# Twelve-tile down projections computed two columns at a time, and the first layer's last two column groups one at a time

## The chip, the cores and the metric

The kernel runs on one core of one Trainium2 chip. The metric is device time in microseconds, the median of several executions. Engines have the profile's names: PE is TensorE (matrix products; PEld its weight loads), DVE is VectorE, ACT is ScalarE, POOL is GpSimd, SP is SyncE, which issues the weight transfers.

## The reference

An encoder trunk of two layers on 256 tokens with 2048 features, all in float32. The first layer mixes tokens by attention, the second by a gated linear recurrence; both end in the same gated feed-forward, which the change is about:

```python
x = x + mixer(rms_norm(x, norm_mix))
x = x + (jax.nn.silu(h @ w_gate) * (h @ w_up)) @ w_down    # h = rms_norm(x, norm_ffn)
# x: 256 x 2048; w_gate, w_up: 2048 x 5632; w_down: 5632 x 2048
```

The second layer's recurrent mixer begins with `rms_norm` of the first layer's result and the projection `h @ w_in`.

## The kernel before

**Products.** Every float32 operand is held as two parts, `hi` and `lo` (the rest). A product of a 128x128 activation tile with a 128x512 weight tile is three matmuls: hi by hi, hi by lo, lo by hi (`product`, L289 to L296). The 256 tokens are two blocks `a` of 128; the accumulator of one block and 512 columns fills one PSUM bank, and the pool `ps_a` has four such banks, handed out in turn.

**Weight tiles.** One weight transfer (`half()`, `load_half`) brings 512 KB: two 128-row slices of 512 columns, which is one *step* of one *column group*. ScalarE casts it to `hi` (L123), VectorE subtracts to get `lo` (L124); there are five buffers each for the raw tile, `hi` and `lo`. One weight tile feeds four products (two slices, two token blocks), that is 12 matmuls of 128x512.

**Pairs.** `project_pair` computes two column groups `j` = 0, 1 together, in a list of steps. A step is a number `n` and the columns it serves: the first steps serve both, one after the other, the last ones first finish column 0 and then column 1, so that column 0's `done` (adding its two banks into the result) runs beside column 1's products. In the steps named in `SEVEN` (2 and 5) both columns' weight tiles are combined and seven products do the work of eight (`seven_forms`, L251 to L274): VectorE makes weight sums (`wx`, L264 to L267), ScalarE and VectorE split them (`wxh` L271, `wxl` L272), and at the end `merge` (L331 to L337) puts four further banks (`pm`, pool `ps_m`) together. The activation sides of these products (`x_forms`, tiles `nf` and `hf`) are prepared when the activation tiles are.

**Feed-forward.** The 5632 hidden features are 44 tiles, computed in parts of 12, 16 and 16 (`PARTS`). For each part, *units* of four hidden tiles are computed first: one pair whose columns are gate and up. A unit's end (L783 to L787, then `turned` and L795, L796) adds the banks, applies SiLU and the product, transposes the block (DVE, L462), copies it together in 16 pieces (ACT, L470: tile `tf` from `tb`) and splits the four hidden tiles (`act`: hi by ACT L795, lo by DVE L796). Then the part's *down projection* adds its share to the residual `x_tok`, in four column groups of 512.

- A sixteen-tile part (eight steps) uses `down`: two pairs (columns 0 and 1, then 2 and 3), with seven products in steps 2 and 5.
- The twelve-tile part (six steps) uses `output`, which is also what the mixers' output projections use: column after column, each by `project_tokens` (matmuls on L247), with two banks per column, all eight products in every step; the result is added on L498.

In the third part the second pair follows `LAST_STEPS`, in which step 3 comes before step 2.

**The end of the first layer.** The third part's `down` also prepares the next norm: as each column is done, `norm.add` squares it on ACT (`nj`, L426), transposes and copies it (L462, L468 on DVE, L470 on ACT; the buffers `tb` and `tf` are single) and writes four operand tiles `xg` (hi ACT L418, lo DVE L419). After the last column, `norm.finish` and `spread` compute the row factors (`nrt`, `nr`, `ndg` L444, a small product L450, the copy `nrb` L452). TensorE meanwhile runs `project_two`: the first two output columns of `w_in`, first over the eight operand tiles of columns 0 and 1, then those of column 2, then those of column 3. Their result passes through a convolution on DVE and ACT (`cb` L827, L829, L832) into `xs` (L378, L379), which the recurrence's gate products read (`pm<-xs,ghi`). The gates' weights (`graw`, L855) are loaded into memory that the feed-forward has just given up; ACT and POOL split them (`ghi` L856, `glo` L857).

**What sets the order.** TensorE's instructions stand in the order of the code. Those of the other engines and of the transfer queue are put in order by a scheduler that plays the program through with its own times; each engine then works strictly in that order.

Of the kernel before, what the change touches and what calls it, by code (L numbers as in the profile page):

```python
# [21 lines left out]
KT = D // P  # L22
# [8 lines left out]
FIRST_STEPS = (0, 1, 3, 4, 2, 6, 5, 7)  # L31
LAST_STEPS = (0, 1, 3, 2, 4, 5, 6, 7)
HALF = 8
# [40 lines left out]
def trunk(ctx, tc, w, out):  # L74
# [64 lines left out]
    def unit_steps(first):  # L139
        return FIRST_STEPS if first else USUAL_STEPS, True  # L140

    def down_steps(p, second):
        last = p == len(PARTS) - 1
        return LAST_STEPS if second and last else USUAL_STEPS, True

    def ffn_order(l):
        units = [wide(f"w_gate{l}"), wide(f"w_up{l}")]
        seq, i = [], 0
        for p, n in enumerate(PARTS):
            for _ in range(n // FOUR):  # L150
                for k, cols in pair_plan(*unit_steps(i == 0)):
# [135 lines left out]

    def project_pair(xs, forms, order, middle, done):
        banks = [[new_acc() for _ in range(2)] for _ in range(2)]  # L289
        begun = set()  # L290

        def product(acc, x, wt, last=False):
            for i, (a, b) in enumerate(((x[0], wt[0]), (x[0], wt[1]), (x[1], wt[0]))):
                pe.matmul(acc, a, b, start=id(acc) not in begun, stop=last and i == 2)  # L294
# [7 lines left out]
        steps = pair_plan(*order)  # L302
        seven = [n for n in order[0] if n in forms]
        for n, cols in steps:
            if n in forms:
                s1, s2, s3, s4 = forms[n]
                b11, b21, t3, b22, t1, t2, t4 = seven_forms()
                if n == seven[0]:
                    p1, q6, q5, q7 = (ps_m.tile([P, WIDE], F32, tag="pm", name=nm("pm")) for _ in range(4))
                last = n == seven[-1]  # L310
                product(p1, tokens(2 * n, 0), b11, last)
                product(banks[0][0], tokens(2 * n + 1, 0), b21)
                product(banks[1][0], s4, b22)
# [3 lines left out]
                product(banks[0][1], tokens(2 * n + 1, 1), t4)  # L317
                if last:
                    middle(p1, q5, q6, q7)
            else:  # L320
                for j in cols:
                    half()
                    hi, lo = (flat(t) for t in newest["tiles"])
                    end = n == order[0][-1]
                    for a in range(2):
                        for k in range(2):
                            product(banks[j][a], tokens(2 * n + k, a), (hi[:, k, :], lo[:, k, :]), end and k == 1)
                    if end:
                        done(j, banks[j])

# [175 lines left out]

    def down(xs, forms, p, norm=None, end=False):
        for c in (0, 2):
# [18 lines left out]

            project_pair(xs, forms, down_steps(p, c > 0), middle, done)
        if norm is not None:
# [245 lines left out]
    def ffn(norm, nxt):  # L775
        def unit(hid, forms, first):
            got = []
# [10 lines left out]

            project_pair(norm.xs, norm.forms, unit_steps(first), lambda *banks: got.extend(merge(*banks)), done)
            u = got[1]  # L790
# [7 lines left out]
            for i, n in enumerate(SEVEN):  # L798
                if forms is not None and first <= 2 * n < len(hid):
                    forms[n] = x_forms(hid[2 * n], hid[2 * n + 1], f"hf{i}")  # L800

        for p, n in enumerate(PARTS):
            hid, forms = [], {} if n == KT else None
            for i in range(n // FOUR):
                unit(hid, forms, p == i == 0)
            last = p == len(PARTS) - 1
            if last and nxt is not None:
                ln_exp_tables()
            if n == KT:
                down(hid, forms, p, nxt if last else None, last and nxt is None)  # L810
            else:
                output(hid)

# [220 lines left out]
```

## Time and profile before

| | |
|---|---|
| median of three runs | 2022.96 us (2022.78 to 2024.07) |
| profiled execution: its own time | 2022.37 us |
| profiled execution: span from first to last instruction | 2020.6 us |
| mean granted clock of TensorE | 0.993 |
| HBM read | 382.13 MB, 190 GB/s over the span |

Rows of the profile that the prediction quotes have these forms. *Waits*: the waiting engine, tile and line, what it waited for; total us, number of waits, longest. *Windows*: start and end from the span's start, length, then busy us (and instructions) of PE, PEld, DVE, ACT, POOL, the granted clock (1.00 is full), the busy share of the DMA engines, GB/s. *Timeline*: start, duration, engine, line, operation, output from inputs, shape, count, and in brackets the idle time before it and what ended it. *Chain*: start, duration and count of one piece of the chain of work that ended last.

### The profile page before, as it was taken

How to read it: one execution, taken by the hardware profiler on the slowest of the kernel's cores; microseconds unless marked ns; L12 is line 12 of the kernel's file. 1: busy time of each engine (PE TensorE's matmuls, PEld its weight loads, DVE VectorE, ACT ScalarE, POOL GpSimd, SP SyncE). 2: the span in 40 equal slices, each digit the busy share in tenths (PEclk: the TensorE clock that was granted, in tenths of full speed). 3: DMA queues.
4: the chain of work that ended last, by engine and by line, in shares of the span. 5: the costliest groups of instructions: out<-in, count | busy, mean ns of one | idle time of the engine just before them, and what ended most of it. 6: DMA issues, size and time to landing. Idle time of an engine off the chain costs nothing.

```text
span 2020.6 us, 27860 instructions
## 1 busy us (share of the span) xinstructions
PE 1995.2 (99%) x9944; PEld 1696.2 (84%) x9944; DVE 1666.0 (82%) x2347; ACT 1320.7 (65%) x2054; POOL 165.7 (8%) x213
## 2 busy tenths in 40 slices
PE   9999999999999999999899999999999999999999
PEld 8898888878888888887799998888788888888887
DVE  8998788856888888889868887898657898878897
ACT  7666666644667546677688898667545766457663
POOL 1463000000000000000133330000000000000000
PEclk9999999999999999999999999999999999999999
DMA  8444665656555665555555555655566566665564
GB/s 320 158 137 140 193 200 187 207 168 198 192 195 187 219 208 188 190 195 192 188 163 188 178 179 174 200 188 187 195 185 202 185 204 206 203 192 187 196 222 146
DMA packets 109004, 386.06 MB, mean 191 GB/s; under 512 B 12225, under 2 KB 12993, under 8 KB 108737
## 3 DMA queue, kind: packets, MB, share of 16 engines
q1 hardware_dynamic: 108720, 384.26, 58.0%
q8 instruction: 78, 1.28, 0.3%
q14 instruction: 62, 0.50, 0.1%
q10 hardware_dynamic: 144, 0.02, 0.0%
HBM read 382.13 MB, written 2.10 MB: 190 GB/s over the span
## 4 chain that ended last, share of the span: by engine, by line
PE 52%; issue 41%; DVE 4%; DMA 1%; ACT 1%; POOL 0%; DVEq 0%; SPq 0%; ACTq 0%; POOLq 0%
PE acc L294 24%; PE acc L247 7%; PE acc L225 6%; PE pm L294 4%; PE acc L341 3%; PE acc L342 3%; PE acc L343 3%; DVE lo L124 2%; PE pm L342 1%; PE pm L343 1%; PE pm L341 1%; DMA raw<-in_w_up_dram 1%; ACT hi L123 0%; DMA graw<-in_w_gates_dram 0%; ACT tf L470 0%
## 5 line engine op out<-in xcount | busy, mean ns | idle before, releaser
L123 ACT CAST hi<-raw 128x1024 fp32r<-128x1024 f32 (+1 forms) x708 | 730.4, 1045 | 486.1 <-PE acc L294 314.1
L124 DVE TENSOR_TENSOR lo<-raw,hi 128x1024 fp32r<-128x1024 f32 (+1 forms) x708 | 857.4, 1228 | 172.0 <-ACT hi L123 169.9
L294 PE MATMUL acc<-hi,xg 128*128 128x512 f32 x2200 | 694.4, 389 | 2.3 <-DVE fg L783 1.2
L294 PEld LDWEIGHTS acc<-hi,xg 128*128 128x128 f32 x2200 | 412.9, 188 | 91.0 <-DVE fg L783 2.0
L294 PE MATMUL acc<-lo,xg 128*128 128x512 f32 x1100 | 427.9, 389 | 0.0
L247 PE MATMUL acc<-hi,act 128*128 128x512 f32 x896 | 283.4, 395 | 6.2 <-ACT act L795 5.4
L294 PE MATMUL acc<-hi,act 128*128 128x512 f32 x800 | 252.7, 389 | 0.0
L294 PEld LDWEIGHTS acc<-lo,xg 128*128 128x128 f32 x1100 | 206.5, 188 | 42.4
L247 PEld LDWEIGHTS acc<-hi,act 128*128 128x128 f32 x896 | 170.7, 191 | 43.8 <-ACT act L795 6.3
L470 ACT COPY tf<-tb 32x256 f32<-32x256 f32 x448 | 180.8, 403 | 12.7 <-DVE tb L462 6.1
L294 PEld LDWEIGHTS acc<-hi,act 128*128 128x128 f32 x800 | 150.2, 188 | 32.3 <-issue 0.7
L247 PE MATMUL acc<-lo,act 128*128 128x512 f32 x448 | 176.8, 395 | 0.0
L294 PE MATMUL acc<-lo,act 128*128 128x512 f32 x400 | 155.6, 389 | 0.0
L342 PE MATMUL acc<-xg,hi 128*128 128x256 f32 x512 | 146.7, 286 | 2.0 <-DVE xg L419 1.9
L341 PE MATMUL acc<-xg,hi 128*128 128x256 f32 x512 | 146.8, 287 | 1.0 <-ACT xg L418 1.0
L343 PE MATMUL acc<-xg,lo 128*128 128x256 f32 x512 | 146.2, 285 | 0.0
L264 DVE TENSOR_TENSOR wx<-raw,raw 128x512 f32<-128x512 f32 x60 | 41.5, 692 | 123.7 <-DMA raw<-in_w_up_dram 97.1
L225 PE MATMUL acc<-xg,hi 128*128 128x512 f32 x384 | 127.1, 400 | 0.5 <-ACT hi L123 0.5
L271 ACT CAST wxh<-wx 128x1536 fp32r<-128x1536 f32 x60 | 88.9, 1482 | 49.6 <-DVE wx L267 46.7
L272 DVE TENSOR_TENSOR wxl<-wx,wxh 128x1536 fp32r<-128x1536 f32 x60 | 104.8, 1747 | 10.5 <-ACT wxh L271 10.5
L342 PEld LDWEIGHTS acc<-xg,hi 128*128 128x128 f32 x512 | 99.7, 195 | 2.5 <-DVE xg L419 2.4
L341 PEld LDWEIGHTS acc<-xg,hi 128*128 128x128 f32 x512 | 99.8, 195 | 1.5 <-ACT xg L418 1.3
(239 smaller groups left out, 2728.4 us busy)
## 6 DMA issues: line engine op xcount, KB each, us to landing
raw<-in_w_gate_dram SPq DMA_DIRECT2D x176, 512.0 KB, 4.0
raw<-in_w_up_dram SPq DMA_DIRECT2D x176, 512.0 KB, 4.4
raw<-in_w_down_dram SPq DMA_DIRECT2D x176, 512.0 KB, 4.2
raw<-in_w_in_dram SPq DMA_DIRECT2D x64, 512.0 KB, 4.6
raw<-in_w_qv_dram SPq DMA_DIRECT2D x40, 512.0 KB, 4.3
raw<-in_w_o_dram SPq DMA_DIRECT2D x32, 512.0 KB, 3.6
raw<-in_w_out_dram SPq DMA_DIRECT2D x32, 512.0 KB, 4.3
graw<-in_w_gates_dram SPq DMA_DIRECT2D x32, 256.0 KB, 3.6
```

The lines of the kernel that those rows point to most:

```text
L123: newest["cast"] = act.copy(hi[:, sl, :], raw[:, sl, :])
L124: dve.tensor_tensor(lo[:, sl, :], raw[:, sl, :], hi[:, sl, :].bitcast(F32), ALU.subtract)
L225: pe.matmul(o, w, x, start=(k == 0 and not part), stop=(k == total - 1 and not part))
L247: pe.matmul(accs[a], x, wt[:, k, :], start=(k0 + k == 0 and n == 0), stop=(end and k == 1 and n == 2))
L264: dve.tensor_tensor(x[:, 0, :], r2[:, 0, :], r1[:, 0, :], ALU.add)
L271: act.copy(xh, x)
L272: dve.tensor_tensor(xl, x, xh[:].bitcast(F32), ALU.subtract)
L294: pe.matmul(acc, a, b, start=id(acc) not in begun, stop=last and i == 2)
L341: pe.matmul(o, hi, x[:, :S], start=start, stop=False)
L342: pe.matmul(o, hi, x[:, S:], start=False, stop=False)
L343: pe.matmul(o, lo, x[:, :S], start=False, stop=stop)
L470: act.copy(o, y)
```

## The change

The twelve-tile part now goes through `down` and `project_pair` as the others do. It has no seven-product steps there (no `x_forms` are prepared for its hidden tiles). Of its six steps the first four serve both columns and the last two (steps 4 and 5) go column by column. In the third part of the first layer the second pair (columns 2 and 3) is computed `alone`: all eight steps of column 2, then all eight of column 3, and with all eight products in each. `LAST_STEPS` is gone, so the same pair in the second layer follows the usual steps, 2 before 3. The order in which weights are fetched (`ffn_order`) follows. Banks are taken from the pool at their first product.

```diff
-LAST_STEPS = (0, 1, 3, 2, 4, 5, 6, 7)
+SHORT = 6
...
-    def pair_plan(steps, apart):
-        m = 1 + steps.index(SEVEN[-1]) if apart else len(steps)
-        return [(n, (0, 1)) for n in steps[:m]] + [(n, (j,)) for j in range(2) for n in steps[m:]]
...
+    def pair_plan(steps, together):
+        return [(n, (0, 1)) for n in steps[:together]] + [(n, (j,)) for j in range(2) for n in steps[together:]]
...
+    def down_plan(n, alone):
+        if alone:
+            return pair_plan(range(n), 0)
+        return pair_plan(range(n), SHORT - 2 if n == SHORT else 1 + SEVEN[-1])
...
             down = wide(f"w_down{l}_{p}")
-            if n != KT:
-                seq += down
-                continue
             for c in range(0, len(down), n):
-                for k, cols in pair_plan(*down_steps(p, c > 0)):
+                for k, cols in down_plan(n // 2, l == 0 and p == len(PARTS) - 1 and c > 0):
                     seq += [down[c + n // 2 * j + k] for j in cols]
...
-    def project_pair(xs, forms, order, middle, done):
-        banks = [[new_acc() for _ in range(2)] for _ in range(2)]
+    def project_pair(xs, forms, plan, middle, done):
+        banks = [[], []]
         begun = set()
+
+        def bank(j, a):
+            while len(banks[j]) <= a:
+                banks[j].append(new_acc())
+            return banks[j][a]
...
-            project_pair(xs, forms, down_steps(p, c > 0), middle, done)
+            alone = norm is not None and c > 0
+            project_pair(xs, {} if alone else forms, down_plan(len(xs) // 2, alone), middle, done)
...
-            if n == KT:
-                down(hid, forms, p, nxt if last else None, last and nxt is None)
-            else:
-                output(hid)
+            down(hid, forms, nxt if last else None, last and nxt is None)
```

**TensorE at the first layer's twelve-tile projection.** The first matmul with each weight tile `hi`, up to the first that reads hidden tile 8 (`act_4332`; `act_3622` is hidden tile 0, `act_3983` tile 6). Before:

```order
L247 MATMUL acc_4344<-hi_4347,act_3622 128x512
...
L247 MATMUL acc_4344<-hi_4365,act_3628 128x512
...
L247 MATMUL acc_4344<-hi_4383,act_3977 128x512
...
L247 MATMUL acc_4344<-hi_4401,act_3983 128x512
...
L247 MATMUL acc_4344<-hi_4419,act_4332 128x512
```

With the change:

```order
L297 MATMUL acc_4350<-hi_4345,act_3622 128x512
...
L297 MATMUL acc_4370<-hi_4365,act_3622 128x512
...
L297 MATMUL acc_4350<-hi_4385,act_3628 128x512
...
L297 MATMUL acc_4370<-hi_4403,act_3628 128x512
...
L297 MATMUL acc_4350<-hi_4421,act_3977 128x512
...
L297 MATMUL acc_4370<-hi_4439,act_3977 128x512
...
L297 MATMUL acc_4350<-hi_4457,act_3983 128x512
...
L297 MATMUL acc_4370<-hi_4475,act_3983 128x512
...
L297 MATMUL acc_4350<-hi_4493,act_4332 128x512
```

Hidden tile 8 is read with the fifth weight tile before and with the ninth now. On ScalarE and VectorE the casts of the four hidden tiles keep their places: two weight casts stand between the sixteen copies and them, as before.

**VectorE from the last column's end in the first layer on** (`x_tok<-x_tok,acc` adds a finished bank; `tb`, `tf` and `xg` belong to the norm of the column). Before, from column 3's second bank:

```order
L522 TENSOR_TENSOR x_tok<-x_tok,acc_8717 128x512
L462 STREAM_TRANSPOSE tb_9077<-x_tok 128x512
L124 TENSOR_TENSOR lo_9320<-raw_9318,hi_9319 128x1024
L462 STREAM_TRANSPOSE tb_9077<-x_tok 128x512
L124 TENSOR_TENSOR lo_9350<-raw_9348,hi_9349 128x1024
L419 SCALAR_TENSOR_TENSOR xg_9023<-tf_9004,pk,xg_9023 128x256
...
L436 TENSOR_REDUCE nrt_9109<-nsq_3278 128x2
L124 TENSOR_TENSOR lo_9393<-raw_9391,hi_9392 128x1024
L468 COPY tf_9078<-tb_9077 32x2x128 x8
L437 TENSOR_SCALAR nrt_9109<-nrt_9109 128x2
L419 SCALAR_TENSOR_TENSOR xg_9097<-tf_9078,pk,xg_9097 128x256
```

With the change:

```order
L524 TENSOR_TENSOR x_tok<-x_tok,acc_8911 128x512
L464 STREAM_TRANSPOSE tb_9050<-x_tok 128x512 x2
L124 TENSOR_TENSOR lo_9293<-raw_9291,hi_9292 128x1024
L470 COPY tf_9051<-tb_9050 32x2x128 x8
L438 TENSOR_REDUCE nrt_9082<-nsq_3278 128x2
L439 TENSOR_SCALAR nrt_9082<-nrt_9082 128x2
L124 TENSOR_TENSOR lo_9323<-raw_9321,hi_9322 128x1024
L421 SCALAR_TENSOR_TENSOR xg_9070<-tf_9051,pk,xg_9070 128x256
```

Before, column 2's operands (`xg_9023` from `tf_9004`) stood between the last column's transposes and its copies; now they stand earlier, and the last column's work follows its add without them.

**ScalarE at the row factors.** Before:

```order
L541 ACTIVATE nr_9112<-rsq_s_9113 128x2
L856 CAST ghi_9294<-graw_9295 128x512
L452 COPY nrb_9249<-pm_9246 128x256
L856 CAST ghi_9300<-graw_9301 128x512
L123 CAST hi_9447<-raw_9446 128x1024
```

With the change:

```order
L123 CAST hi_9365<-raw_9364 128x1024
L544 ACTIVATE rsq_s_9086<-nrt_9082 128x2
L544 ACTIVATE nr_9085<-rsq_s_9086 128x2
L856 CAST ghi_9267<-graw_9268 128x512
L856 CAST ghi_9273<-graw_9274 128x512
L454 COPY nrb_9222<-pm_9219 128x256
L123 CAST hi_9420<-raw_9419 128x1024
```

Both of the first two gate casts now stand ahead of the copy `nrb`, where there was one.

More of the change, by code (lines that the diff above doesn't have):

```diff
@@ L316, in project_pair @@
                 product(q6, s2, t2, last)
[L317 removed]
+                product(bank(0, 1), tokens(2 * n + 1, 1), t4)
                 if last:
                     middle(p1, q5, q6, q7)
[L320 to L329 removed]
+                continue
+            end = n == plan[-1][0]
+            for j in cols:
+                half()
+                hi, lo = (flat(t) for t in newest["tiles"])
+                for a in range(2):
+                    for k in range(2):
+                        product(bank(j, a), tokens(2 * n + k, a), (hi[:, k, :], lo[:, k, :]), end and k == 1)
+                if end:
+                    done(j, banks[j])
     def merge(p1, q5, q6, q7):
@@ L775, in ffn, with unit @@
     def ffn(norm, nxt):
-        def unit(hid, forms, first):
+        def unit(hid, forms, parts, first):
             got = []
```

30 lines of the change are left out of this document (13 added, 17 removed).

## The prediction

> **What bounds the kernel.** I read the page's first part, then the waits of TensorE over the whole span, then windows and timelines around each of those waits. First the page: the span and each engine's busy time, its share of the span and its instructions.
>
> ```profile
> span 2020.6 us, 27860 instructions
> PE 1995.2 (99%) x9944; PEld 1696.2 (84%) x9944; DVE 1666.0 (82%) x2347; ACT 1320.7 (65%) x2054; POOL 165.7 (8%) x213
> ```
>
> TensorE (PE) is busy for all but 2020.6 - 1995.2 = 25.4 us. So there are two ways to a shorter time: fewer products, or less of what TensorE loses to waits and to a lowered clock (a slow product counts as busy). Who waited for whom on TensorE (us in total, times, longest):
>
> ```profile
> PE acc L247 <- ACT act L795: 5.4, 2, 2.7
> PE pm L294 <- DVE wxl L272: 2.2, 1, 2.2
> PE acc L342 <- DVE xg L419: 1.9, 1, 1.9
> PE pm L341 <- DVE xs L378: 1.8, 1, 1.8
> PE pm L341 <- ACT hi L123: 1.7, 1, 1.7
> PE acc L294 <- DVE fu L786: 1.2, 4, 0.4
> PE pm L450 <- DVE ndg L444: 1.1, 1, 1.1
> PE acc L247 <- DVE act L796: 0.8, 2, 0.5
> ```
>
> The first and last rows are the twelve-tile down projections (L247 reads `act`, the hidden tiles that L795 and L796 write), once in each layer. The wxl, xg, ndg and xs rows all lie at the end of the first layer. Those are the two places that the change touches.
>
> **The twelve-tile projections.** The windows view gives the two stretches from their first product to the next unit's first (length; busy time of PE, weight loads, VectorE, ScalarE and GpSimd with instructions; granted clock; DMA), and the stretch just behind the wait. The chain of waits gives the undisturbed pace (start, length, products).
>
> ```profile
> 395.59:467.53 71.94, 68.70 (x289) 55.82 (x288) 39.87 (x44) 33.64 (x45) 0.00 (x0) 0.95 0.55 172
> 1436.98:1508.83 71.85, 68.89 (x289) 55.92 (x288) 39.84 (x44) 33.61 (x45) 0.00 (x0) 0.95 0.55 172
> 409.70:416.50 6.80, 6.26 (x15) 4.46 (x14) 3.20 (x6) 2.46 (x4) 0.00 (x0) 0.50 0.66 228
> 1963.08 27.88 PE acc L294 x123
> ```
>
> A product of 128x512 follows another every 27.88 / 123 = 0.2267 us. 288 of them (4 columns x 6 weight tiles x 12) need 65.29 us; the stretches took 71.94 and 71.85. So each loses 6.65 and 6.56 us, **13.2 us** together, twice what the waits view shows as idle: after a wait of 2.7 us the granted clock is 0.50 for 6.8 us. The timeline shows the wait and its suppliers.
>
> ```profile
> 406.25 0.39 PE L247 MATMUL acc<-hi,act 128*128 128x512 f32 x1
> 409.34 0.51 PE L247 MATMUL acc<-hi,act 128*128 128x512 f32 x1 [2.71 <-ACT act L795]
> 395.34 1.28 DVE L786 TENSOR_TENSOR fu<-acc,fu 128x512 f32<-128x512 f32 x2
> 400.33 6.63 ACT L470 COPY tf<-tb 32x256 f32<-32x256 f32 x16 [0.72 <-DVE tb L462]
> 408.89 1.32 ACT L795 CAST act<-tf 128x256 fp32r<-128x256 f32 x4
> 410.11 1.04 ACT L123 CAST hi<-raw 128x1024 fp32r<-128x1024 f32 x1
> 411.69 1.22 DVE L124 TENSOR_TENSOR lo<-raw,hi 128x1024 fp32r<-128x1024 f32 x1
> ```
>
> The last unit ends at 395.6, and its four hidden tiles need VectorE, sixteen copies and four casts of ScalarE, and are whole some 16 us later. Column by column, TensorE has four weight tiles of other work, 4 x 12 x 0.2267 = 10.9 us, and stands at 406.5. By pairs it has eight, 21.8 us, and asks for hidden tile 8 at 417.4. ScalarE's and VectorE's orders keep the same kinds of work in the same places up to there, so the tiles arrive as before; the ninth weight tile, last in line, is whole at 411.69 + 1.22 = 412.9. That leaves 4.5 us, and the loss of 13.2 us goes, its half-clock stretch with it: nothing is late next. No product is added here. The cover is those four extra weight tiles; without them the 6.6 us per layer come back.
>
> Here the Trainium skill speaks otherwise ("TensorE: Matmul & The Clock Gate", section "Why this matters for your kernels"): it asks for no idle gaps of TensorE beyond about 3 us, since one whole idle window is what halves the clock. By that rule a wait of 2.7 us halves nothing and its removal would be worth the idle time alone, 5.4 + 0.8 = 6.2 us. The trace differs: its row behind a 2.71 us wait has clock 0.50, and the measured length of the two stretches decides.
>
> What pairs add is the handover of accumulators: a pair holds all four, and its second column starts 2.72 us after the previous pair's last product, needing the two buffers that this product filled. VectorE must have added them to `x_tok` by then, and what queues behind a late add on VectorE are the weights' `lo` parts. Three handovers per layer are of this kind (unit to pair, pair to pair, pair to unit). The nearest rows: units handing over to what follows lost 1.2 us in 4 waits (L786, 0.4 at most); the pairs of the sixteen-tile projections have no row of their own among TensorE's waits. From 0 to 6 x 0.4 = 2.4 us; I take **0.4 us**, nearer to the sixteen-tile pairs, since VectorE is busy 39.87 of 71.94 us here.
>
> **The end of the first layer.** Each row's idle time and its ender stand in brackets; the windows are the stretch from the projection's end to the second gate product, two at half clock, and one of undisturbed 256-wide products behind them.
>
> ```profile
> 951.43 0.39 PE L294 MATMUL pm<-wxh,hf 128*128 128x512 f32 x1
> 954.01 0.50 PE L294 MATMUL pm<-wxl,hf 128*128 128x512 f32 x1 [2.19 <-DVE wxl L272]
> 977.04 0.28 PE L341 MATMUL acc<-xg,hi 128*128 128x256 f32 x1
> 985.17 0.38 PE L342 MATMUL acc<-xg,hi 128*128 128x256 f32 x1 [1.91 <-DVE xg L419]
> 1008.58 0.58 PE L341 MATMUL pm<-xs,ghi 128*128 128x256 f32 x1 [1.82 <-DVE xs L378]
> 992.64 6.96 SPq L855 DMA_DIRECT2D graw<-in_w_gates_dram  x4
> 977.04:1008.58 31.54, 23.63 (x158) 22.02 (x157) 25.05 (x53) 20.96 (x43) 5.80 (x12) 0.87 0.50 160
> 986.54:989.95 3.41, 3.04 (x15) 2.75 (x14) 3.26 (x9) 3.02 (x8) 0.00 (x0) 0.50 0.68 225
> 1007.02:1013.85 6.83, 5.19 (x22) 4.89 (x23) 6.35 (x11) 3.16 (x5) 1.56 (x5) 0.50 0.64 205
> 1013.90:1030.00 16.10, 16.10 (x137) 16.10 (x137) 6.44 (x10) 13.02 (x25) 6.82 (x9) 1.00 0.43 134
> ```
>
> Three terms. (a) The seven-product steps of the last two columns go, and with them the weight sums that TensorE awaited: 954.01 - 951.43 - 0.23 = **2.35 us** gained (0 if VectorE is late with something else instead). (b) Two steps of seven products become eight: 2 x 3 matmuls x 0.2267 = **1.36 us** lost. (c) From the projection's last product (977.04) the next stage waits for the normed operands, then for the gates' weights, whose transfer reuses the feed-forward's memory and starts at 992.64, 15.60 us after the end and 0.4 us after the last operand; the second gate product follows 15.94 us behind it, 31.54 us after the end.
>
> In the change the third column is finished eight weight tiles (21.8 us) before the end, so its norm work is out of the way and the fourth column's runs alone. Durations for that chain:
>
> ```profile
> 980.58 0.69 DVE L522 TENSOR_TENSOR x_tok<-x_tok,acc 128x512 f32<-128x512 f32 x1
> 975.13 1.30 DVE L462 STREAM_TRANSPOSE tb<-x_tok 128x512 f32<-128x512 f32 x2
> 973.52 0.63 ACT L426 ACTIVATE nj<-x_tok 128x512 f32<-128x512 f32 x1 [0.66 <-DVE x_tok L522]
> 974.05 0.18 ACT L426 ACTIVATION_READ_ACCUMULATOR nj<-x_tok 128x1 f32 x1
> 976.47 3.31 ACT L470 COPY tf<-tb 32x256 f32<-32x256 f32 x8 [0.53 <-DVE tb L462]
> 979.80 1.05 ACT L123 CAST hi<-raw 128x1024 fp32r<-128x1024 f32 x1
> 990.56 1.69 DVE L419 SCALAR_TENSOR_TENSOR xg<-tf,pk,xg 128x256 fp32r<-128x256 f32 x4 [0.43 <-ACT xg L418]
> 996.52 0.37 ACT L452 COPY nrb<-pm 128x256 f32<-128x256 f32 x1
> ```
>
> By ScalarE's new order, counted from the last product: a weight cast that waits for it (to 1.15), two squares with their read-outs (1.6, to 2.8), eight copies (3.3, to 6.1), another cast (to 7.2), the operands' upper parts. VectorE's add and transposes (0.69 + 1.30) end at 2.2, inside that. Its `lo` part of the cast (1.22, to 8.4) and four operand parts (1.69) end at 10.1; with the same 0.4 the gates' transfer starts at 10.5 instead of 15.6, and the second gate product comes at 26.4 instead of 31.5. **5.1 us** gained. The bounds: nothing but a loss of 0.6 (two gate casts instead of one now stand ahead of the `nrb` copy on ScalarE) if the chain is no shorter, and at most 31.5 - 18.6 = 12.9 us, since the 158 products in between need 158 x 16.10 / 137 = 18.6 us without any wait. I take the chain's sum, as each link has a row. Behind it before ran 5.3 us at half clock; I leave that as it was.
>
> In the last layer the same projections swap two steps; VectorE's order there becomes that of the sixteen-tile projection before it, which has no wait row on TensorE. I cost it at 0; the cover is VectorE's slack, and if it is gone the price is that of the wxl wait, 2.35 us.
>
> The sum: 13.2 - 0.4 + 2.35 - 1.36 + 5.1 = 18.9 us. The profiled execution took 2022.37 us (span 2020.6), so 2003.5; the runs' median of 2022.96 lies 0.59 above it, so **2004.1 us**.
>
> **Rivals.** (1) *The end of the layer gives nothing*: the relief is eaten where VectorE and ScalarE serve the norm, and the wait stands before `ndg` or the gates; only the added products remain. For it: five waits in a row lie there, so freeing one exposes the next. Against: two sets of weight sums, their `wxl` parts and a merge leave VectorE in that stretch. 2022.96 - 13.2 + 0.4 + 1.36 = 2011.5 us. (2) *The clock stays up behind the shorter waits*: half of the last 5.3 us at 0.50 comes back too, 2.6 us: 2001.5 us. Against it, the 1.91 us wait at 985.17 is followed by a 0.50 row at 986.54. By the Trainium skill's rule above ("TensorE: Matmul & The Clock Gate"), which would halve nothing under 3 us, this is what happens; the trace does not bear it out. (3) *The hidden tiles are no earlier in time for the pairs*, so that the change does not do what it says there: only the end of the layer gains, 2.35 - 1.36 + 5.1 = 6.1, and 2016.9 us. The 4.5 us of room speak against it. (4) *Slower: accumulator handovers.* If VectorE's adds come more than 2.72 us late at the six handovers, each wait costs what a wait of 2.7 us costs now, clock included: 6.6 us. From three of them on (19.8 us against 19.3 gained without them) the kernel is no faster; with four it takes 2022.96 - 19.3 + 26.4 = 2030.1 us. For it: handovers with waits exist (L786). Against: 0.4 us at most there. The Trainium skill ("TensorE: Matmul & The Clock Gate", section "A second HAM failure mode: psum-queue depth-cycling") describes such losses when accumulator banks cycle; the sixteen-tile pairs here cycle the same way without a wait row.
>
> **How the numbers follow.** Forecast 0.67, (1) 0.13, (2) 0.08, (3) 0.03, (4) 0.07, and 0.02 for gains and losses that cancel. A measurement of this kernel tells 0.2% (4 us) from no change; the forecast and (1) to (3) are all beyond that: faster 0.91, same 0.02, slower 0.07. The range reaches from 1999, the forecast with (2) and a chain 2.5 us shorter still, to 2012, which takes in (1).
>
> **What would show it.** In the profile of the change the two twelve-tile stretches should last 65.3 to 66.5 us at clock 1.00, with no wait for `act`; longer ones with waits for `x_tok` mean (4), for `act` (3). No wait for `wxl` should stand in the first layer's last projection. The gates' transfer should start 10 to 11 us after that projection's last product and the second gate product at 26 to 27; a start after 15 us means (1), and a clock of 1.00 right behind means (2). The forecast is wrong if the twelve-tile stretches keep more than 3 us of loss each, or if the second gate product comes 31 us after the end as before.

## The result, and the profile after

The changed kernel takes 2005.61 us (median of 4 runs, 2002.79 to 2005.76), the kernel before 2022.87 us beside it: a ratio of 0.9912, 95% interval 0.9895 to 0.9929. The forecast was 2004.1 us. The same program once more in a later set (the repeat, below) took 2001.66 us (2001.18 to 2002.99), a ratio of 0.9892 (0.9876 to 0.9908); a fourth run of it, at 2464.62 us and a granted clock of 0.752, was disturbed and is left out here and below.

The profiled execution took 2005.76 us. The page's first rows, span and busy time:

```profile
span 2004.0 us, 27854 instructions
PE 1985.7 (99%) x9950; PEld 1688.8 (84%) x9950; DVE 1649.0 (82%) x2329; ACT 1317.1 (66%) x2051; POOL 167.8 (8%) x213
```

TensorE is busy for all but 18.3 us now (25.4 before). Who waited for whom on TensorE:

```profile
PE pm L343 <- DVE xs L380: 3.9, 2, 2.3
PE acc L297 <- DVE fu L789: 3.1, 5, 1.3
PE pm L452 <- DVE ndg L446: 2.2, 1, 2.2
PE acc L297 <- DVE fg L786: 1.1, 2, 0.6
```

The rows for `act` and `wxl` are gone, and so are those for `xg`; `fu` and `fg`, the adds with which VectorE empties the banks of a unit's gate and up columns, together went from 2.4 to 4.2 us. The windows of the changed kernel (start and end, length, busy us of PE, PEld, DVE, ACT, POOL, clock, DMA): the two twelve-tile stretches, layer 0's last projection, from its last product to the second gate product, from there to the mixer's output projection, and the sixteen-tile stretches of both layers, which the change hardly touches.

```profile
395.56:460.84 65.28, 65.28 (x289) 54.05 (x288) 38.16 (x43) 32.69 (x44) 0.00 (x0) 1.00 0.58 187
1425.32:1490.60 65.28, 65.28 (x289) 54.05 (x288) 38.28 (x43) 32.69 (x44) 0.00 (x0) 1.00 0.58 186
...
885.03:971.13 86.10, 85.97 (x379) 70.87 (x378) 74.90 (x109) 63.20 (x105) 0.00 (x0) 1.00 0.61 200
971.13:997.20 26.07, 19.72 (x158) 18.92 (x156) 19.14 (x42) 17.08 (x33) 5.92 (x12) 0.97 0.57 187
997.20:1210.78 213.58, 213.57 (x1767) 213.40 (x1768) 172.58 (x282) 190.43 (x323) 77.83 (x98) 0.99 0.55 173
460.84:885.03 424.19, 422.77 (x1861) 348.77 (x1860) 358.63 (x431) 262.40 (x350) 0.00 (x0) 1.00 0.60 199
1490.60:2004.00 513.40, 507.52 (x2233) 418.20 (x2231) 427.48 (x514) 305.77 (x404) 0.00 (x0) 1.00 0.58 194
```

The same windows of the kernel before that the prediction did not show:

```profile
889.89:977.04 87.15, 84.92 (x373) 69.67 (x372) 82.95 (x115) 62.20 (x98) 0.00 (x0) 1.00 0.58 196
1008.58:1222.23 213.65, 213.57 (x1767) 213.27 (x1768) 172.03 (x283) 189.02 (x322) 76.17 (x97) 0.99 0.55 173
467.53:889.89 422.36, 422.11 (x1861) 349.00 (x1860) 357.13 (x431) 261.87 (x350) 0.00 (x0) 1.00 0.61 199
1508.83:2020.60 511.77, 507.06 (x2233) 418.44 (x2231) 427.02 (x513) 305.11 (x404) 0.00 (x0) 1.00 0.58 194
```

So, of the 16.6 us between the two spans: the twelve-tile stretches gave 6.66 + 6.57 = 13.2, the last projection 1.05, the chain behind it 31.54 - 26.07 = 5.5, together 19.7. The sixteen-tile stretches took back 424.19 - 422.36 = 1.83 and 513.40 - 511.77 = 1.63, and the rest of the program gave 0.3.

The timeline shows the end of layer 0: the first product after the projection, the waits of TensorE, then the last links of the chain to the gates on ScalarE and VectorE, and the gates' transfer.

```profile
971.13 0.28 PE L343 MATMUL acc<-xg,hi 128*128 128x256 f32 x1
...
982.86 0.71 PE L452 MATMUL pm<-ndg,ones 128*128 128x128 f32 x4 [2.21 <-DVE ndg L446]
994.52 0.35 PE L343 MATMUL pm<-xs,ghi 128*128 128x256 f32 x1 [2.32 <-DVE xs L380]
997.21 0.58 PE L343 MATMUL pm<-xs,ghi 128*128 128x256 f32 x1 [1.56 <-DVE xs L380]
```

```profile
976.99 1.05 ACT L123 CAST hi<-raw 128x1024 fp32r<-128x1024 f32 x1
978.07 1.23 DVE L124 TENSOR_TENSOR lo<-raw,hi 128x1024 fp32r<-128x1024 f32 x1 [0.81 <-ACT hi L123]
979.21 1.67 DVE L421 SCALAR_TENSOR_TENSOR xg<-tf,pk,xg 128x256 fp32r<-128x256 f32 x4
980.98 0.80 SPq L855 DMA_DIRECT2D graw<-in_w_gates_dram  x2
```

The transfer starts 980.98 - 971.13 = 9.85 us after the last product (15.60 before), the second gate product 26.08 us after it.

### The profile page after: what moved, and what is told of

Its sections match the earlier page's. It is cut to its first block, busy times and chain, and to the rows that moved or that the text cites. A ratio compares the mean times of both kernels' runs of the same rounds, so it can differ in the third digit from the quotient of the medians.

```text
span 2004.0 us, 27854 instructions
## 1 busy us (share of the span) xinstructions
PE 1985.7 (99%) x9950; PEld 1688.8 (84%) x9950; DVE 1649.0 (82%) x2329; ACT 1317.1 (66%) x2051; POOL 167.8 (8%) x213
## 4 chain that ended last, share of the span: by engine, by line
PE 48%; issue 41%; DVE 6%; DMA 3%; ACT 1%; POOL 0%; SPq 0%; DVEq 0%; ACTq 0%; POOLq 0%
PE acc L297 26%; PE acc L245 4%; PE pm L297 3%; PE acc L223 3%; PE acc L343 3%; PE acc L344 3%; PE acc L345 3%; DVE lo L124 3%; DMA raw<-in_w_up_dram 1%; PE pm L343 1%; PE pm L345 1%; PE pm L344 1%; DMA x_tok<-in_xt_dram 1%; ACT hi L123 0%; DMA raw<-in_w_k_dram 0%
## 5 line engine op out<-in xcount | busy, mean ns | idle before, releaser
L472 ACT COPY tf<-tb 32x256 f32<-32x256 f32 x448 | 180.7, 403 | 10.1 <-DVE tb L464 4.4
L262 DVE TENSOR_TENSOR wx<-raw,raw 128x512 f32<-128x512 f32 x58 | 40.2, 692 | 127.5 <-DMA raw<-in_w_up_dram 98.6
L297 PEld LDWEIGHTS acc<-lo,act 128*128 128x128 f32 x606 | 113.7, 188 | 23.4
L245 PEld LDWEIGHTS acc<-hi,act 128*128 128x128 f32 x512 | 96.1, 188 | 19.7
L343 PEld LDWEIGHTS acc<-xg,hi 128*128 128x128 f32 x512 | 98.6, 193 | 0.0
```

The source lines that it names most:

```text
L245: pe.matmul(accs[a], x, wt[:, k, :], start=(k0 + k == 0 and n == 0), stop=(end and k == 1 and n == 2))
L262: dve.tensor_tensor(x[:, 0, :], r2[:, 0, :], r1[:, 0, :], ALU.add)
L343: pe.matmul(o, hi, x[:, :S], start=start, stop=False)
L472: act.copy(o, y)
```

## The experiments

Each was timed in five rounds beside the kernel before on the same chip; the changed kernel's row is the result above. The last three columns are from each run's trace: the lengths of the two twelve-tile stretches, and the start of the gates' transfer and of the second gate product, both counted from the end of layer 0's last down projection.

| run | median us (range) | ratio to before, 95% | twelve-tile, us | gates' transfer | second gate product |
|---|---|---|---|---|---|
| changed kernel | 2005.61 (2002.79 to 2005.76) | 0.9895 to 0.9929 | 65.28, 65.28 | 9.85 | 26.08 |
| twelve-tile pairs alone | 2008.46 (2007.83 to 2012.79) | 0.9916 to 0.9942 | 65.28, 65.28 | 15.18 | 30.91 |
| single columns alone | 2015.29 (2012.49 to 2018.08) | 0.9948 to 0.9973 | 69.31, 70.35 | 9.85 | 26.64 |
| no step in pairs | 2015.48 (2013.36 to 2019.49) | 0.9953 to 0.9976 | 70.94, 70.71 | 9.85 | 26.77 |
| one step in pairs | 2007.65 (2006.64 to 2007.93) | 0.9910 to 0.9935 | 66.60, 66.58 | 9.85 | 26.35 |
| repeat | 2001.66 (2001.18 to 2002.99) | 0.9876 to 0.9908 | 65.28, 65.28 | 9.84 | 25.64 |
| pair at the layer's end | 2008.09 (2007.36 to 2009.43) | 0.9911 to 0.9936 | 65.28, 65.28 | 13.77 | 32.00 |
| adds first | 2110.30 (2106.28 to 2113.66) | 1.0418 to 1.0448 | - | - | - |
| filler | 2000.55 (1999.31 to 2001.98) | 0.9872 to 0.9899 | 65.28, 65.28 | 9.84 | 25.54 |
| old step order kept | 2003.28 (2001.68 to 2003.41) | 0.9881 to 0.9916 | 65.28, 65.28 | 9.84 | 26.78 |
| two fillers, six buffers | 2002.44 (2001.35 to 2004.55) | 0.9883 to 0.9913 | 65.28, 65.28 | 9.84 | 27.12 |
| before, filled | 2016.28 (2014.77 to 2017.54) | 0.9951 to 0.9978 | 69.31, 69.30 | 16.09 | 29.80 |
| two fillers | 2003.78 (2002.77 to 2004.44) | 0.9886 to 0.9919 | 65.28, 65.28 | 9.85 | 26.75 |

### The two parts apart

**Twelve-tile pairs alone.** Against the changed kernel:

```diff
-    def down_plan(n, alone):
-        if alone:
-            return pair_plan(range(n), 0)
-        return pair_plan(range(n), SHORT - 2 if n == SHORT else 1 + SEVEN[-1])
+    def down_plan(n, last):
+        steps = (0, 1, 3, 2, 4, 5, 6, 7) if last else range(n)
+        return pair_plan(steps, SHORT - 2 if n == SHORT else 1 + SEVEN[-1])
...
```

> Only the twelve-tile pairs; the last projections of both layers are as before. If the parts add up, the two twelve-tile stretches last 65.3 us each at clock 1.00 (13.2 us together gone) and layer 0's end keeps its 31.5 us from the projection's last product to the second gate product: 2009.7 us, or up to 2013 if the units behind the pairs lose the 3.4 us that they lose in the whole change. If the pairs needed the shorter end of the layer (rival), the time stays above 2016.

Measured 2008.46 us, with both stretches at 65.28 us and the old chain (15.18 and 30.91 us). The pairs need nothing from the other part; the time lies 1.2 us under the expected lower end.

**Single columns alone.** The twelve-tile part goes through `output` again, and the last layer keeps its old step order:

```diff
...
-            down(hid, forms, nxt if last else None, last and nxt is None)
+            if n == KT:
+                down(hid, forms, nxt if last else None, last and nxt is None)
+            else:
+                output(hid)
```

> Only layer 0's last two column groups by themselves; twelve-tile projections column by column as before. If the parts add up: the wait for wxl gone (2.35), six products added (1.36), the chain to the second gate product 26.1 us instead of 31.5 (5.4): 6.4 us, so 2016.5 us, and the twelve-tile stretches keep 71.9 us. If the chain is only shorter because everything ran earlier (rival): 31 us in the chain and 2021.9 us.

Measured 2015.29 us and 26.64 us in the chain: it is shorter by itself, not because the program ran earlier. One thing was not as expected: the twelve-tile stretches took 69.31 and 70.35 us in place of 71.9, with the same wait of 2.71 us in them. That is taken up below. The gains of the two parts in their medians, 14.9 and 8.1 us, sum to 23.0; the whole gave 17.3 and, in the repeat, 22.1. With ranges of 2 to 6 us, and of 6 to 9 us for the kernel before, this neither shows nor excludes an interaction; the stretches and the chain in the table show none.

### The cover of the hidden tiles

The number of twelve-tile steps done in pairs was set to 0 and to 1 in place of 4:

```diff
-        return pair_plan(range(n), SHORT - 2 if n == SHORT else 1 + SEVEN[-1])
+        return pair_plan(range(n), 0 if n == SHORT else 1 + SEVEN[-1])
```

> The whole change, but the twelve-tile plan goes column by column through the same new code (no step in pairs). Cover theory: TensorE asks for the third unit's tiles after four weight tiles again, waits 2.7 us in each layer, the clock halves behind it when most of the wait lies in one clock window: 2.9 to 6.6 us per layer, 2011.4 to 2018.8 us. If the new code itself (accumulators taken late) made the gain, it stays at 2005.6 us.

> As the whole change, but only the first step of the twelve-tile plan is in pairs: TensorE asks for the third unit's tiles after five weight tiles, 13.6 us into the stretch instead of 10.9 or 21.8. Cover theory: the tiles come 13.7 to 14 us in, so a wait of 0 to 0.5 us and no halved clock: 2005.6 to 2007 us. If the pairs are needed as such (rival: the wait is set by the casts in line, whole at 17.3 us), a wait of about 3 us with the clock behind it: 2012 to 2019 us.

With no step in pairs 2015.48 us. The loss is back, although everything runs through the new code:

```profile
394.87:465.81 70.94, 67.49 (x290) 55.05 (x288) 39.92 (x44) 33.62 (x45) 0.00 (x0) 0.98 0.56 176
1430.55:1501.26 70.71, 67.26 (x290) 54.93 (x289) 39.78 (x44) 33.57 (x45) 0.00 (x0) 0.98 0.55 176
```

With one step, which puts a single weight tile more ahead of hidden tile 8, 2007.65 us. The window and the only wait in its first twelve-tile stretch:

```profile
394.74:461.34 66.60, 65.86 (x289) 53.90 (x288) 39.04 (x44) 32.82 (x45) 0.00 (x0) 1.00 0.58 182
```

```profile
409.97 0.73 PE L297 MATMUL acc<-hi,act 128*128 128x512 f32 x2 [0.74 <-DVE act L799]
```

The wait of 2.7 us is gone; what is left is 0.74 us for a lower part (0.2 us more than the upper end expected, and the median is 0.7 us above its). So it is the cover that works, and 2.72 us of it were most of what was needed. The rival, that the ninth weight tile in line sets the time, falls.

### Which half of the edit shortens the chain

Columns 2 and 3 of layer 0 as a pair, but with all eight products:

```diff
...
-            project_pair(xs, {} if alone else forms, down_plan(len(xs) // 2, alone), middle, done)
+            project_pair(xs, {} if alone else forms, down_plan(len(xs) // 2, False), middle, done)
```

> As the whole change, but layer 0's last two column groups are a pair (six steps together, the last two by column) with all products. It tells the two halves of the edit apart: without weight sums the wait for wxl is gone, but the third column ends only two weight tiles before the end, so its norm work stands ahead of the fourth's. If the single columns shorten the chain: the second gate product at 30 to 32 us behind the last product, 2009 to 2011.5 us. If the missing weight sums do it: 26 us and 2005.6 us.

Measured 2008.09 us. In its timeline the last projection's end is at 969.98; the gates' transfers as they are issued, the landing of the first in the chain that ended last, then TensorE:

```profile
983.75 9.24 SPq L855 DMA_DIRECT2D graw<-in_w_gates_dram  x4
983.75 5.55 DMA graw<-in_w_gates_dram
```

```profile
980.91 0.39 PE L343 MATMUL acc<-xg,hi 128*128 128x256 f32 x1 [2.14 <-ACT xg L420]
...
1001.98 0.58 PE L343 MATMUL pm<-xs,ghi 128*128 128x256 f32 x1 [1.95 <-DVE xs L380]
```

The wait for `xg` is back and the second gate product comes 32.00 us after the end, as late as before. So the single columns shorten the chain: with them the third column's norm work is done before the fourth ends. The split is less clean than these two numbers say. The transfer starts at 13.77 us here, 1.83 us earlier than the 15.60 before, so without the weight sums not only the wait for `wxl` goes; but the first of the gates' transfers took 5.55 us to land (3.28 before, 3.80 in the changed kernel), so that it was there 19.32 us after the end, against 18.88 before. Of the 5.75 us by which the changed kernel's transfer starts earlier, 3.92 us are thus shown for the single columns. Why that transfer took longer, in this one trace, stays open.

### The clock, and the wait that it follows

Layer 0's twelve-tile stretch in the run with single columns alone has the old wait of 2.71 us (it ends at 408.58), but no lowered clock; layer 1's has the same wait (it ends at 1441.72) and a lowered clock. Windows of the two stretches, and of pieces of 3.41 us round each wait:

```profile
394.83:464.14 69.31, 65.86 (x290) 53.92 (x289) 39.84 (x44) 33.62 (x45) 0.00 (x0) 1.00 0.58 183
1427.97:1498.32 70.35, 67.14 (x289) 54.70 (x288) 39.82 (x44) 33.60 (x45) 0.00 (x0) 0.98 0.56 177
...
404.38:407.80 3.42, 1.49 (x7) 0.91 (x5) 0.50 (x1) 3.35 (x7) 0.00 (x0) 1.00 0.01 2
407.80:411.21 3.41, 1.89 (x7) 1.28 (x8) 3.41 (x7) 2.59 (x6) 0.00 (x0) 1.00 0.43 136
```

```profile
1438.62:1442.03 3.41, 0.70 (x3) 0.30 (x2) 1.58 (x2) 3.37 (x7) 0.00 (x0) 1.00 0.01 2
1442.03:1445.45 3.42, 2.92 (x7) 1.84 (x6) 3.26 (x6) 1.51 (x3) 0.00 (x0) 0.50 0.68 217
```

The pieces are not chosen by hand. In each of the 14 traces, all changes of the granted clock lie a whole number of 3.413 us apart (in the kernel before, 409.69 and 1450.755 are 305.0 of them apart). Cut at these lines, a wait counts by how much of it falls into one window. In the first stretch the line at 407.80 splits the wait, the windows hold 1.93 and 1.52 us of idle time, and the clock stays; in the second one window holds 3.41 - 0.70 = 2.71 us, and the next has clock 0.50. The changed kernel shows the same in one place: of its waits of 2.21 and 2.32 us only the second lowers the clock.

```profile
978.63:982.04 3.41, 2.01 (x17) 1.81 (x16) 3.41 (x7) 2.26 (x6) 0.20 (x4) 1.00 0.45 135
982.04:985.45 3.41, 2.60 (x22) 2.60 (x23) 0.85 (x5) 0.60 (x1) 0.00 (x0) 1.00 0.74 252
992.28:995.69 3.41, 0.86 (x3) 0.48 (x3) 3.41 (x7) 2.56 (x4) 1.70 (x3) 1.00 0.72 219
995.69:999.11 3.42, 1.90 (x7) 1.73 (x8) 3.39 (x7) 0.57 (x1) 0.13 (x2) 0.50 0.79 260
```

I counted the windows of all 14 traces in this way, behind the first 13 us of each (clock full, over 0.5 us in which the trace has no product running). With up to 1.68 us of idle time none of 77 was followed by clock 0.50; with 1.69 to 1.93 us, 12 of 17; from 1.94 us on, all 35. Back to full speed it takes a window with hardly any idle time: of windows at half clock, all 41 with under 0.25 us were the last one, and all 13 with over 0.55 us were followed by another (between, 3 of 9).

**Before, filled.** To take the clock from the wait without moving the wait, TensorE got 11 products to compute in it that nobody reads:

```diff
+            if len(xs) == 12 and k0 == 8 and newest.pop("first", None):
+                spare = ps_m.tile([P, WIDE], F32, tag="pm", name=nm("pm"))
+                for _ in range(11):
+                    pe.matmul(spare, xs[0][:, :P], xs[1], start=True, stop=True)
...
+                newest["first"] = True
                 output(hid)
```

> The kernel before, with 11 unread 128x512 products (2.49 us) in each twelve-tile projection where it waits for the third unit's tiles. If half of the loss is the clock: no 0.50 behind the wait, the stretches last 65.3 + 2.9 + 0.5 to 0.7 = 68.7 to 69 us in place of 71.9, and the median is 2018 to 2020 us. If the clock is not set by TensorE's idle time: 71.9 us and 2023 us.

Measured 2016.28 us, and in the trace, window and timeline:

```profile
395.05:464.36 69.31, 68.35 (x301) 55.96 (x300) 39.02 (x44) 32.89 (x45) 0.00 (x0) 1.00 0.56 176
```

```profile
405.93 2.65 PE L244 MATMUL pm<-act,act 128*128 128x512 f32 x11
408.80 0.50 PE L251 MATMUL acc<-hi,act 128*128 128x512 f32 x1 [0.21 <-ACT act L799]
```

The tiles come no earlier and products were added, and yet each stretch is 2.6 us shorter than before, the length that the wait has without a lowered clock (69.31 as above, where the window lines split it). That is 0.3 us more than expected, and the median 1.7 us under the expected lower end (in its trace the chain to the gates, which this edit does not touch, was 1.7 us shorter, 29.80 against 31.54). The clock follows TensorE's idle time. The wait proper costs 69.31 - 65.28 = 4.0 us in each layer, the clock up to 2.6 more.

**Filler at the gates.** The same means in the changed kernel, where the clock falls behind the wait for `xs`:

```diff
                 o = pst[:, j * S : (j + 1) * S]
                 for k in range(2):
+                    if b == g == j == k == 0:
+                        for _ in range(18):
+                            pe.matmul(pst[:, S:], nr.xs[0][:, :P], nr.xs[1][:, :S], start=True, stop=True)
```

> As the whole change, with 18 products of 128x256 that nobody reads ahead of the first gate product of layer 1 (18 x 0.12 = 2.16 us, inside the 2.3 us for which TensorE waits there). If the wait is what halves the clock: clock 1.00 behind it. What that brings is at most 3.4 us (6.8 us at half clock): 2002.2 us; if the stretch behind is paced by ScalarE and VectorE, nothing: 2005.6 us. If the clock halves for another reason, 0.50 stays behind it.

Measured 2000.55 us, the lowest of all; its timeline, and the window from the second gate product to the mixer's output projection:

```profile
991.55 2.32 PE L880 MATMUL pm<-xg,xg 128*128 128x256 f32 x18
994.70 0.38 PE L343 MATMUL pm<-xs,ghi 128*128 128x256 f32 x1 [0.47 <-DVE xs L380]
```

```profile
994.70:1206.13 211.43, 211.35 (x1768) 211.16 (x1769) 172.39 (x282) 189.02 (x322) 76.78 (x97) 1.00 0.56 175
```

The clock is 1.00, and from the last down product to the mixer's output projection it takes 25.54 + 211.43 = 236.97 us, against 239.65 in the changed kernel and 238.56 in the repeat. So 1.6 to 2.7 us come back. The medians agree (2001.66 for the repeat on the same chip), but the ranges of the two overlap, so the gain is shown by the trace and not by the times.

**Two fillers.** Also 17 such products ahead of the norm's transposing products:

```diff
+                for _ in range(17):
+                    pe.matmul(pst[:, :S], nr.xs[0][:, :P], nr.xs[1][:, :S], start=True, stop=True)
                 for a in range(2):
                     sl = slice(a * P, a * P + P)
```

> As the filler run (18 unread products ahead of the first gate product), and 17 more of them (2.04 us) ahead of the norm's transposing products, where TensorE waits 2.2 us for ndg. If only the clock counts: no 0.50 is left after the start, and the 1.7 us that a half-clock window of 3.4 us costs come back: 1998.5 to 1999.5 us. If ScalarE and VectorE pace the stretch up to the gates, TensorE only comes to its next wait earlier and stands there longer: 2000 to 2001 us, as the filler run.

Measured 2003.78 us. No 0.50 follows the wait for `ndg`, but TensorE comes earlier to the gates and stands there:

```profile
988.21 2.32 PE L882 MATMUL pm<-xg,xg 128*128 128x256 f32 x18
991.75 0.35 PE L343 MATMUL pm<-xs,ghi 128*128 128x256 f32 x1 [1.23 <-DVE xs L380]
...
994.06 0.38 PE L343 MATMUL pm<-xs,ghi 128*128 128x256 f32 x1 [0.84 <-DVE xs L380]
```

The second gate product comes 26.75 us after the end, not earlier than without (25.54), and these waits lower the clock in their turn. Up to the gates, ScalarE and VectorE set the pace; a faster TensorE only waits longer. That is the rival; the time is even above what it expected, with 2.7 us of waits for `x_tok` and `fu` (0.7 in the run with one filler).

### The small waits in the units

**Repeat.** The changed kernel, unchanged.

> The changed kernel once more, for its spread and a second trace. If the 3.4 us that the unchanged units lost are chance in single transfers, the small waits for fu and fg stand in other units and their sum moves by 1 us or more; if they follow from the program, the same units wait again within 0.3 us each. If clock windows lie by chance over the program, some runs lie about 3 us below the others, as 2002.8 beside 2005.7.

The repeat's waits for the units' last banks, and its sixteen-tile stretches:

```profile
PE acc L297 <- DVE fg L786: 1.0, 2, 0.5
PE acc L297 <- DVE fu L789: 0.9, 3, 0.5
```

```profile
460.19:882.83 422.64, 422.38 (x1861) 348.87 (x1860) 358.32 (x432) 262.85 (x350) 0.00 (x0) 1.00 0.60 199
1487.07:1999.40 512.33, 507.25 (x2233) 418.34 (x2231) 428.02 (x514) 306.07 (x404) 0.00 (x0) 1.00 0.59 194
```

The same program takes 422.64 and 512.33 us in these stretches here, 424.19 and 513.40 in the first trace. The 2.6 us between the two executions lie mostly in the waits for `fu` (3.1 and 0.9 us): most of what the first trace seemed to give back differs from execution to execution of the same program. Where it comes from is seen on VectorE, which awaits a weight transfer (for the sums `wx`, L262) ahead of the adds that free the banks. In 12 traces (all but adds first and six buffers; without the first units of a layer, behind which TensorE waits in every trace) there are 654 such transfers. 523 landed within 5.0 us, and TensorE waited for `fu` or `x_tok` behind 8 of them; 71 took 5.3 us or more, and it waited behind 30; of the 60 between, behind 6. The first sum's transfer at 535.29 in the changed kernel took 5.84 us and cost 0.64 us, its twin in the repeat 5.45 us and 0.25 us. Why some take longer was not tried.

**Adds first.** The sums may not pass the adds:

```diff
-            dve.tensor_tensor(x[:, 0, :], r2[:, 0, :], r1[:, 0, :], ALU.add)
+            i = dve.tensor_tensor(x[:, 0, :], r2[:, 0, :], r1[:, 0, :], ALU.add)
+            if newest.get("adds") is not None:
+                follow(i, newest.pop("adds"))
...
-                        dve.tensor_tensor(u[:, a, :], acc, u[:, a, :], ALU.add)
+                        newest["adds"] = dve.tensor_tensor(u[:, a, :], acc, u[:, a, :], ALU.add)
```

> As the whole change, but in each unit VectorE's sums of weights for the first seven-product step may not stand ahead of the previous unit's adds that free the accumulators. If the small waits (fu and fg, 4.2 us in all) come from a late weight transfer that VectorE awaits ahead of those adds: they go, 2001.5 to 2003 us. If VectorE is simply behind with its work: they stay or grow, 2005.6 us or more; the sums could also come too late for TensorE (waits for wxl, 2008 us or more).

A clear miss as a remedy: 2110.30 us. TensorE's longest waits:

```profile
PE pm L299 <- ACT wxh L271: 42.4, 20, 2.4
PE pm L299 <- DVE wxl L272: 25.6, 20, 1.3
```

Waits for `fu` and `fg` are gone altogether, as the theory has it, but the sums now come too late in 20 units, 68.0 us of waiting with the clock behind some of it. So the order on VectorE does decide these waits, and the order that the scheduler had chosen, sums first, is the better one by far.

**Two fillers, six buffers.** As two fillers, and a sixth buffer for arriving weights:

```diff
-        raw = wp.tile([P, HALF, P], F32, tag="raw", name=nm("raw"), bufs=5)
+        raw = wp.tile([P, HALF, P], F32, tag="raw", name=nm("raw"), bufs=6)
```

> As the whole change, with 17 unread 128x256 products ahead of the norm's transposing products and 18 ahead of the first gate product, and six buffers in place of five for arriving weights. If the small waits in the units come from transfers that land late and a transfer may start earlier with a sixth buffer: they go, but for the 0.5 us at the start of each layer, and no 0.50 clock is left behind the start: 1997 to 2000 us. If the buffers do not set when transfers start: the waits stay (0.7 to 4 us a run) and the time is that of the filler run, 2000 to 2001 us; if transfers started earlier only share the memory with others and land later, it is slower than that.

Measured 2002.44 us. One wait for `fu` is left (0.98 us), though five transfers took over 5.3 us; but the two at the layers' starts (`fg`) took 1.2 us each (0.6 and 1.1 us with two fillers alone), and the gates were waited for as with two fillers. The two runs are of different chips and their ranges overlap, so the sixth buffer is not shown to gain anything.

### The swapped steps of the last layer

**Old step order kept**, in the last layer's last pair alone:

```diff
-        return pair_plan(range(n), SHORT - 2 if n == SHORT else 1 + SEVEN[-1])
+        return pair_plan((0, 1, 3, 2, 4, 5, 6, 7) if last else range(n), SHORT - 2 if n == SHORT else 1 + SEVEN[-1])
...
```

> As the whole change, but the last layer's last pair keeps the old order of its steps (3 before 2). If the swap is worth nothing: the time of the changed kernel on this chip within 1 us (2002 to 2006 us), and the stretch from the last down projection's start to the end within 0.5 us of the 89.3 us of the changed kernel. If the old order is better or worse on VectorE: a wait for wxl or the accumulators there and 2.4 us of difference.

Measured 2003.28 us. From the last projection's first product to the end it took 88.3 us, against 89.3 in the changed kernel and 88.4 in the repeat, and there is no wait for `wxl`. That is 0.5 us under the lower end expected, and as in the repeat; the swap is worth nothing that these runs can tell.

## Why the prediction was right

**The twelve-tile stretches** (13.2 us forecast): 13.23 us in the two traces, no wait for `act`, clock 1.00, as the text asked. The cause, four hidden tiles asked for too early, is shown from both sides by 0 and 1 steps in pairs. The size was luck. The text took the halved clock behind a 2.7 us wait as certain, since both rows of the one trace had it. In the runs with single columns alone and with no step in pairs the same wait cost 4.0, 5.1, 5.4 and 5.7 us, by where the 3.413 us lines fell; before, both layers happened to have the most seen, 6.6 and 6.7. The term should have been a range, 8.1 to 13.3 us.

**The handovers** (0.4 us, 0 to 2.4): nothing at the six places, since both stretches need just the 65.28 us of their products and the next unit's first products do not wait; rival (4) has no row there. The text's argument that the sixteen-tile pairs cycle their accumulators without a wait row holds for the trace that it had and for the changed kernel's first; in 8 of the 14 traces there is one, for `x_tok`, with waits of 0.2 to 1.6 us. But the text left the rest of the layers behind them at nothing, and there the first trace lost 3.5 us and the repeat 0.8, mostly behind transfers that landed late. That is the step that was missing: of the 18.9 us forecast, 16.6 appeared in the first trace, though each named term came out at its size or above. In the repeat's trace the difference of spans is 21.2 us.

**The last projection** (2.35 gained, 1.36 lost): 87.15 to 86.10 us, 1.05 against 0.99.

**The chain to the gates** (5.1 us): 5.5 us. The sum fits link by link: the second weight cast ended 6.9 us after the end (7.2 forecast), its `lo` part 8.2 (8.4), the last operand 9.8 (10.1); transfer at 9.85 against 10.5, second gate product at 26.08 against 26.4. The reason given, the third column's norm work out of the way, is shown by the pair at the layer's end: without single columns the transfer starts 3.92 us later and the second gate product comes at 32.00 us. The other reason, named against rival (1), fewer sums on VectorE, goes with the other 1.83 us. The faster clock in this stretch (0.97, before 0.87) is not the cause: with two fillers it was 1.00 there, and the second gate product came at 26.75. That the forecast came within 0.4 us of it is in part luck, for the chain differs between executions: 29.80 to 31.54 us in the three traces with the old order there, 25.64 to 26.78 in the six with the new one and no filler, so the term was worth 3.0 to 5.9 us.

**The swap** (0): nothing to be told from the spread.

**Rival (2)**, the clock stays up behind the shorter waits, is neither right nor wrong: it depends on the execution. In the first trace the clock fell for 6.83 us at the gates (995.69 to 1002.52), in the repeat for 3.41 us there and 3.41 us behind the wait for `ndg`. Where it did not fall at the gates, in the run with the filler, 1.6 to 2.7 us came back, of the 2.6 named. The text's dispute with the Trainium skill ("TensorE: Matmul & The Clock Gate", section "Why this matters for your kernels") was right in its result, waits well under 3 us do halve the clock, and wrong in making of it a rule for each wait.

## What to carry to other kernels

A wait of TensorE of about 2 to 3 us has two prices, the wait itself and a lowered clock behind it that depends on where the wait falls; a term read from one trace should carry both as a range. One more weight tile of other work ahead of the late operand paid for most of the two waits; look for that first, before a faster producer. A product that nobody reads keeps the clock up in a wait that cannot be removed, but only pays where TensorE sets the pace behind it.

## What the runs showed of the hardware that was not expected

- In these traces the granted clock changes only on lines 3.413 us apart. About half a window of idle time (1.69 to 1.93 us) can be enough to halve it for the next window, 1.94 us or more always were, and it stays halved until a window with less than about 0.25 to 0.55 us of idle time. The Trainium skill ("TensorE: Matmul & The Clock Gate", section "What's actually happening") has a free-running window of 3413 ns, which these traces bear out, and says that the half rate comes after at least one idle window, which they do not: half an idle window did it in 12 of 17 cases, 57% of one or more in all 35.
- The runs of the kernel before, in all sets, lie between 2017.9 and 2027.1 us, about twice as wide as those of the changed one (2001.2 to 2005.8). Its two twelve-tile waits, which can halve the clock or not, account for up to 5.2 us of it. For 36 of these runs the mean granted clock is known: the 7 with 0.991 or 0.992 have a median of 2025.1 us, the 8 with 0.995 or 0.996 one of 2021.1 us. So the clock goes along with the time, but not alone: within the 8 the times go from 2017.9 to 2026.5 us.
- 512 KB transfers of weights that land in 4.3 us (median) took up to 6.8 us now and then behind the first 60 us, in other places in each execution of the same program.
